# One more step between score products and value products in the mLSTM and retention chunks of a two-layer hybrid block

## The chip, the cores and the metric

The kernel runs on one core of a Trainium2 chip (trn2). The metric is device microseconds for one launch. TensorE multiplies matrices into PSUM, VectorE (DVE), ScalarE (ACT) and GpSimd (POOL) compute element by element, SyncE (SP) issues most of the DMAs. Each engine takes its own queue of instructions in the order in which it stands, and semaphores tie the queues to each other.

## The reference

Two layers of a block with three branches over 512 tokens of 1024 features, in fp32: an mLSTM, a sparse latent attention and a retention, each projected, gated and added, then a gated feed-forward. What the change touches are the chunks of 128 tokens of two branches:

```python
def mlstm step(carry, inp):                      # per chunk of 128 tokens, 4 heads
    sc = einsum('bhld,bhrd->bhlr', qc, kc) * w_intra
    num = einsum('bhlr,bhrv->bhlv', sc, vc) + w_inter * einsum('bhld,bhdv->bhlv', qc, c_st)
    out = num / max(|den|, exp(-m_row))
    c_new = decay * c_st + einsum('bhl,bhld,bhlv->bhdv', wk, kc, vc)

def retention step(state, inp):
    sc = einsum('bhld,bhrd->bhlr', qc, kc) * intra
    out = einsum('bhlr,bhrv->bhlv', sc, vc) + q_decay * einsum('bhld,bhdv->bhlv', qc, state)
    state = chunk_decay * state + einsum('bhrd,hr,bhrv->bhdv', kc, k_decay, vc)

hm = head_layer_norm(mlstm(...)) * sigmoid(m_o)
hr = head_layer_norm(retention(...)) * silu(r_g)
y = sigmoid(g_m) * (hm @ p_m) + sigmoid(g_a) * (ha @ p_a) + sigmoid(g_r) * (hr @ p_r)
```

## The kernel before, in words

The large products of the block are cut into **sections**: 512 columns of a weight matrix against all 512 tokens, in four PSUM banks named mm. A weight chunk of 256 rows is loaded by SyncE (L235) and split into a rounded high part (whi, ScalarE, L237) and the rest (wlo, VectorE, L238); three matmuls (L255 to L257) then make one product of nearly fp32 accuracy. A section with tokens on the output's partitions (`tok_section`) takes 24 matmuls per weight chunk and ends when its four banks are emptied: for RQ and RK, the query and key of the retention, by ScalarE into rz (L518); a section with features on the partitions (`feat_section`) for a gate by VectorE into sg (L487).

The smaller work of the branches runs **beside** these sections. A branch is a Python generator that issues instructions up to a `yield`; a section calls `tick` twice per weight chunk, and each tick advances a generator by its rate: the mLSTM by 0.75 steps per tick beside RQ, RK and RV (L536), the retention by 1.25 beside the first gate section GM (L562), each drained before the sections after them. Inside a branch four chunks of 128 tokens follow each other one step apart:

```python
def wave(gens, lag=1):
    active, gens, n = [], list(gens), 0
    while active or gens:
        if gens and n % lag == 0:
            active.append(gens.pop(0))
        n += 1
        for g in list(active):
            if next(g, active) is active:
                active.remove(g)
        yield
```

One step of an mLSTM chunk makes the score products (L854), masks them on VectorE into msc (L856) and makes the state product in two halves (L864, both in one PSUM tile), which VectorE adds to the old state (L866, once per half). The next step makes the value products (L877, and L879 against the state), divides by the normalizer (L881 to L884) and normalizes per head (`head_norm`): statistics on VectorE (L361, L362), an addition and a power on GpSimd (L312, L313), four L366 and a multiplication L368 on VectorE, all in place on mhx. Two empty steps later `to_T` turns the chunk with four transposes (L373) into one PSUM tile, which ScalarE rounds (L307) and VectorE subtracts (L308) into hmT, the operand of the projection p_m. The retention does the same with a step of its own ahead for its transposed query and key (L905, L907), with msc named rsc (L915), the products L913, L920, L930 and L932, a copy rhx (L934) and hrT.

The instructions of each engine are then put in order by a scheduler that goes by its own priorities; the code gives the dependencies, and a weight chunk's split and a section's evacuation are issued at high priority. Small PSUM tiles (sm) rotate over four banks. Beside the mLSTM also runs the top-k selection of the attention, pairs of L653 and L654 on VectorE (named top and mask).

Of the kernel before, what the change touches and what calls it, by code (L numbers as in the profile page):

```python
# [77 lines left out]
# [10 lines that stand above are left out]
# [17 lines left out]
class Block:  # L105
# [737 lines left out]
    def mlstm(self, qz, kT, v1, og, hmT):  # L843
        nc = self.nc
        W, G, qw, kw, dec = self.ml
        for v, x in enumerate(self.branch_T("hmT")):
            hmT[v] = x
        states = [None]

        def chunk(c):  # L850
            s = slice(c * 128, (c + 1) * 128)
            p = self.sm([128, 4, 128])
            for h in range(4):
                nc.tensor.matmul(p[:, h, :], lhsT=kT[h // 2][:, s], rhs=qz[:, h, s], start=True, stop=True)  # L854
            sc = self.r("msc", [4, 128])
            nc.vector.tensor_mul(sc, p, W[:, c])  # L856
            cst = states[c]
            if c < NT - 1:
                u = self.sm([128, 2, 129])
                new = self.r("mst", [2, 129])  # L860
                for hp in range(2):
                    for i in range(2):
                        h = 2 * hp + i
                        nc.tensor.matmul(u[:, hp, :], lhsT=kw[c][:, h, :], rhs=v1[:, c, h, :], start=i == 0, stop=i == 1)  # L864
                    if c:
                        nc.vector.scalar_tensor_tensor(new[:, hp, :], cst[:, hp, :], dec[:, hp, c:c + 1], u[:, hp, :],  # L866
                                                       op0=OP.mult, op1=OP.add)
                if c == 0:
                    nc.vector.tensor_copy(new, u)
                states.append(new)  # L870
            yield
            hx = self.r("mhx", [4, 128])
            for hp in range(2):
                o = self.sm([128, 2, 129])
                for i in range(2):
                    h = 2 * hp + i
                    nc.tensor.matmul(o[:, i, :], lhsT=sc[:, h, :], rhs=v1[:, c, h, :], start=True, stop=c == 0)  # L877
                    if c:
                        nc.tensor.matmul(o[:, i, :], lhsT=qw[:, h, s], rhs=cst[:, hp, :], start=False, stop=True)  # L879
                dn = self.stat(2, "mdn")  # L880
                nc.vector.tensor_tensor(dn, o[:, :, 128], G[:, 1, c, 2 * hp:2 * hp + 2], op=OP.max)  # L881
                nc.vector.scalar_tensor_tensor(dn, o[:, :, 128], -1.0, dn, op0=OP.mult, op1=OP.max)
                nc.vector.reciprocal(dn, dn)
                nc.vector.tensor_mul(hx[:, 2 * hp:2 * hp + 2, :], o[:, :, 0:128],  # L884
                                     dn[:, :, None].to_broadcast([128, 2, 128]))
            self.head_norm(hx, og[c])
# [3 lines that stand above are left out]
            self.to_T(hx, hmT, c)  # L890

        yield from wave(chunk(c) for c in range(NT))

    def retention(self, rq, rk, rv, rg, hrT):
        nc = self.nc
        for v, x in enumerate(self.branch_T("hrT")):
            hrT[v] = x
        states = [None]

        def chunk(c):  # L900
            T2 = []
            for n, x in (("rqT", rq), ("rkT", rk)):
                p = self.sm([128, 4, 128])
                for h in range(4):
                    nc.tensor.transpose(p[:, h, :], x[c][:, h, :], self.ident)  # L905
                y = self.r(n, [4, 128])
                nc.scalar.activation(y, p, AF.Copy)  # L907
                T2.append(y)
            qT, kT = T2
            yield  # L910
            p = self.sm([128, 4, 128])
            for h in range(4):
                nc.tensor.matmul(p[:, h, :], lhsT=kT[:, h, :], rhs=qT[:, h, :], start=True, stop=True)  # L913
            sc = self.r("rsc", [4, 128])
            nc.vector.tensor_mul(sc, p, self.c01[:, None, :].to_broadcast([128, 4, 128]))  # L915
            st = states[c]
            if c < NT - 1:
                u = self.sm([128, 4, 128])
                for h in range(4):
                    nc.tensor.matmul(u[:, h, :], lhsT=rk[c][:, h, :], rhs=rv[c][:, h, :], start=True, stop=True)  # L920
                new = self.r("rst", [4, 128])
                if c:
                    nc.vector.tensor_add(new, u, st)
                else:
                    nc.vector.tensor_copy(new, u)
                states.append(new)
            yield
            o = self.sm([128, 4, 128])
            for h in range(4):
                nc.tensor.matmul(o[:, h, :], lhsT=sc[:, h, :], rhs=rv[c][:, h, :], start=True, stop=c == 0)  # L930
                if c:
                    nc.tensor.matmul(o[:, h, :], lhsT=qT[:, h, :], rhs=st[:, h, :], start=False, stop=True)  # L932
            hx = self.r("rhx", [4, 128])
            nc.scalar.activation(hx, o, AF.Copy)  # L934
            self.head_norm(hx, rg[c])
# [3 lines that stand above are left out]
            self.to_T(hx, hrT, c)  # L939

        yield from wave(chunk(c) for c in range(NT))

    def ffn(self, l, X, act):
# [94 lines left out]
```

## Time and profile before

| what | value |
|---|---|
| median of three runs | 1820.44 us (1819.31 to 1820.54) |
| the profiled execution | 1819.63 us |
| its span in the profile | 1817.8 us |
| TensorE busy | 1789.1 us, 98% |
| VectorE busy | 981.1 us, 54% |
| ScalarE busy | 741.4 us, 41% |
| GpSimd busy | 218.8 us, 12% |

The span runs from the first instruction to the last; the execution's own time also has what lies around it. A wait is read in the timeline as the idle time in brackets behind a row, with the instruction that ended it. The mLSTM chunks of the first layer run from 133 to 175 us, the retention chunks from 237 to 273 us; in the second layer from 1031 to 1072 and from 1136 to 1172 us.

### The profile page before, as it was taken

What the parts mean: (1) busy time and instruction counts of PE and PEld (TensorE: products, weight loads), DVE (VectorE), ACT (ScalarE), POOL (GpSimd) and SP (SyncE); (2) the same over time, 40 slices, a digit from 0 to 9 for tenths busy, and PEclk for the clock granted to TensorE, in tenths of its full rate; (3) what the DMA queues carried; (4) which work ended last, traced back from release to release, by engine and by line L of the source; (5) the groups of instructions that cost most, each with busy time, mean ns of one, the idle gap of its engine ahead of it and who ended that gap; (6) DMA issues with size and microseconds to landing.
All of it is one profiled execution on the core that took longest, in us unless ns stands there. A gap on an engine that the chain in (4) does not pass through costs nothing.

```text
span 1817.8 us, 22873 instructions
## 1 busy us (share of the span) xinstructions
PE 1789.1 (98%) x8720; PEld 1491.1 (82%) x8720; DVE 981.1 (54%) x1799; ACT 741.4 (41%) x1208; POOL 218.8 (12%) x274
## 2 busy tenths in 40 slices
PE   9999999999999999999999999999999999999998
PEld 6878888878888888888887788888888888888886
DVE  5698985455545333322357999754546443333223
ACT  5572235656434323322246523366654333223221
POOL 3112240121000000000020132311210000000000
PEclk9999999999999999999999999999999999999999
DMA  6522323222235333222342223232223243332232
GB/s 188 203 83 81 115 72 100 89 91 87 81 128 162 93 95 102 93 96 102 102 131 70 76 85 101 68 112 80 90 70 137 87 158 95 94 105 93 94 103 81
DMA packets 126845, 185.95 MB, mean 102 GB/s; under 512 B 12256, under 2 KB 71136, under 8 KB 126736
## 3 DMA queue, kind: packets, MB, share of 16 engines
q1 hardware_dynamic: 125408, 178.98, 31.4%
q0 software_dynamic: 1184, 5.26, 0.8%
q8 instruction: 68, 1.11, 0.2%
q14 instruction: 41, 0.34, 0.1%
q10 hardware_dynamic: 144, 0.26, 0.0%
HBM read 177.64 MB, written 6.84 MB: 101 GB/s over the span
## 4 chain that ended last, share of the span: by engine, by line
PE 79%; DVE 13%; ACT 3%; issue 2%; DMA 2%; POOL 1%; SPq 0%; POOLq 0%; ACTq 0%; DVEq 0%
PE mm L255 23%; PE mm L257 23%; PE mm L256 23%; DVE wlo L238 3%; DVE mask L654 3%; DVE top L653 2%; PE sm L735 2%; PE sm L714 1%; PE sm L728 1%; ACT whi L237 1%; DVE ru L527 1%; PE sm L373 1%; PE sm L255 0%; PE sm L256 0%; DVE mhx L366 0%
## 5 line engine op out<-in xcount | busy, mean ns | idle before, releaser
L238 DVE TENSOR_TENSOR wlo<-raw,whi 128x1024 fp32r<-128x1024 f32 (+2 forms) x302 | 373.7, 1238 | 585.2 <-ACT whi L237 585.0
L237 ACT ACTIVATE whi<-raw 128x1024 fp32r<-128x1024 f32 (+2 forms) x302 | 314.0, 1040 | 709.1 <-PE mm L256 301.2
L255 PE MATMUL mm<-hT,whi 128*128 128x512 f32 (+1 forms) x1216 | 465.5, 383 | 0.1
L256 PE MATMUL mm<-hT,whi 128*128 128x512 f32 (+1 forms) x1216 | 460.4, 379 | 1.1 <-DVE hT L308 1.1
L257 PE MATMUL mm<-hT,wlo 128*128 128x512 f32 (+1 forms) x1216 | 460.9, 379 | 0.0
L257 PEld LDWEIGHTS mm<-hT,wlo 128*128 128x128 f32 x1216 | 228.8, 188 | 42.9
L256 PEld LDWEIGHTS mm<-hT,whi 128*128 128x128 f32 x1216 | 229.0, 188 | 42.0 <-DVE hT L308 1.7
L255 PEld LDWEIGHTS mm<-hT,whi 128*128 128x128 f32 x1216 | 229.0, 188 | 40.7 <-ACT rg L548 0.5
L255 PE MATMUL mm<-whi,hT 128*128 128x512 f32 (+1 forms) x448 | 177.0, 395 | 1.6 <-ACT hT L307 0.9
L257 PE MATMUL mm<-whi,hT 128*128 128x512 f32 (+1 forms) x448 | 174.8, 390 | 0.0
L256 PE MATMUL mm<-wlo,hT 128*128 128x512 f32 (+1 forms) x448 | 174.2, 389 | 0.0
L255 PEld LDWEIGHTS mm<-whi,hT 128*128 128x128 f32 x448 | 84.2, 188 | 18.7 <-ACT hT L307 1.6
L257 PEld LDWEIGHTS mm<-whi,hT 128*128 128x128 f32 x448 | 84.1, 188 | 18.0 <-issue 1.2
L256 PEld LDWEIGHTS mm<-wlo,hT 128*128 128x128 f32 x448 | 84.2, 188 | 16.1 <-issue 0.5
L325 POOL TENSOR_SCALAR rs<-ms 128x1 f32<-128x1 f32 x16 | 5.7, 354 | 620.4 <-ACT hn L323 620.4
L255 PE MATMUL mm<-whi,fa 128*128 128x512 f32 x192 | 74.7, 389 | 0.0
L256 PE MATMUL mm<-wlo,fa 128*128 128x512 f32 x192 | 74.7, 389 | 0.0
L257 PE MATMUL mm<-whi,fa 128*128 128x512 f32 x192 | 74.7, 389 | 0.0
L716 POOL TENSOR_TENSOR cmb<-tb,mask 128x256 f32<-128x256 f32 (+2 forms) x48 | 51.4, 1075 | 160.0 <-PE sm L728 54.5
L255 PE MATMUL mm<-whi,fr 128*128 128x512 f32 x160 | 62.4, 390 | 0.0
L257 PE MATMUL mm<-whi,fr 128*128 128x512 f32 x160 | 62.3, 389 | 0.0
L256 PE MATMUL mm<-wlo,fr 128*128 128x512 f32 x160 | 62.3, 389 | 0.0
(287 smaller groups left out, 2651.7 us busy)
## 6 DMA issues: line engine op xcount, KB each, us to landing
raw<-w_in SPq DMA_DIRECT2D x104, 512.0 KB, 3.6
raw<-w_gate SPq DMA_DIRECT2D x96, 256.0 KB, 2.8
raw<-w_up SPq DMA_DIRECT2D x96, 256.0 KB, 3.0
raw<-w_down SPq DMA_DIRECT2D x44, 512.0 KB, 3.5
raw<-w_out SPq DMA_DIRECT2D x16, 512.0 KB, 3.6
x<-x SPq DMA_DIRECT2D x8, 512.0 KB, 6.3
rot<-c_rot SPq DMA_DIRECT2D x16, 256.0 KB, 3.0
tb<-bias_dram SPq DMA_DIRECT2D x16, 256.0 KB, 3.8
```

What stands on the lines that cost most here:

```text
L237: nc.scalar.activation(h, r, AF.Copy)
L238: nc.vector.tensor_sub(o, r, h.bitcast(F32))
L255: t.matmul(out, lhsT=A[0], rhs=B[0], start=start, stop=False)
L256: t.matmul(out, lhsT=A[0], rhs=B[1], start=False, stop=False)
L257: t.matmul(out, lhsT=A[1], rhs=B[0], start=False, stop=stop)
L373: self.nc.tensor.transpose(p[:, h, :], x[:, h, :], self.ident)
L527: nc.vector.tensor_mul(u, z, sin)
L653: nc.vector.max(m8, acc)
L654: nc.vector.match_replace(acc, m8, acc, TAKEN)
L714: nc.tensor.matmul(p, lhsT=q[v][:, b * 128:(b + 1) * 128], rhs=kk[v][:, 0:SP], start=v == 0, stop=v == 1)
L716: nc.gpsimd.tensor_add(c, tb[:, T - S:T], masks[b] if b else self.neg)
L735: nc.tensor.matmul(o[:, b, :], lhsT=PT[:, s, :], rhs=V[s][:, h * 64:(h + 1) * 64], start=s == 0, stop=s == b)
```

## The change

Each chunk function gets one more `yield` between the step that makes the scores and the state and the step that makes the value products. Within a branch, one more set of score and state products is issued ahead of a chunk's value products; the branch takes one step more in all.

```diff
                     nc.vector.tensor_copy(new, u)
                 states.append(new)
             yield
+            yield
             hx = self.r("mhx", [4, 128])
             for hp in range(2):
                 o = self.sm([128, 2, 129])
@@ -924,6 +925,7 @@
                 else:
                     nc.vector.tensor_copy(new, u)
                 states.append(new)
+            yield
             yield
             o = self.sm([128, 4, 128])
             for h in range(4):
```

No engine gets more or fewer instructions; lines below the first added one count one higher in the changed kernel, below the second two. What the scheduler makes of it is shown at two places. In the rows, numbers behind a name are allocation counters; the chunks' normalized tiles are mhx_1358, 1422, 1512 and 1590 for mLSTM chunks 0 to 3 before, and mhx_1387, 1473, 1544 and 1604 in the change.

TensorE, first layer, mLSTM, end of the section RQ (mm_1284 to 1287) and start of RK (mm_1690 on), before:

```order
L257 MATMUL mm_1287<-whi_1566,hT11_125 128x512
L373 MATMUL sm_1643<-cm_84,mhx_1422 128x128 x4
L255 MATMUL mm_1690<-whi_1695,hT00_122 128x512
L256 MATMUL mm_1690<-wlo_1696,hT00_122 128x512
L257 MATMUL mm_1690<-whi_1695,hT10_124 128x512
```

Chunk 1's transposes stand there alone; chunk 2's stand 24 weight matmuls into RK, chunk 3's 12 further. The same place in the change (RK is mm_1683 on):

```order
L878 MATMUL sm_1615<-v1_430,msc_1517 128x129
L880 MATMUL sm_1615<-mst_1430,qw_1181 128x129
L373 MATMUL sm_1719<-cm_84,mhx_1473 128x128 x4
L373 MATMUL sm_1748<-cm_84,mhx_1544 128x128 x4
L255 MATMUL mm_1683<-whi_1688,hT00_122 128x512
L256 MATMUL mm_1683<-wlo_1689,hT00_122 128x512
L257 MATMUL mm_1683<-whi_1688,hT10_124 128x512
```

Chunk 3's value products (L878, L880) and the transposes of chunks 1 and 2 now stand right before RK's first matmul; between chunk 2's value products and its transposes stand 12 weight matmuls, chunk 0's transposes, chunk 3's value products and chunk 1's transposes.

ScalarE at the same place, before (sm_1583 and sm_1643 hold the transposed chunks 0 and 1):

```order
L307 ACTIVATE hmT0_1320<-sm_1583 128x4x128
L518 ACTIVATE rz_1656<-mm_1284 128x512
L518 ACTIVATE rz_1660<-mm_1285 128x512
L237 ACTIVATE whi_1781<-raw_1780 128x1024
L518 ACTIVATE rz_1664<-mm_1286 128x512
L518 ACTIVATE rz_1668<-mm_1287 128x512
L307 ACTIVATE hmT0_1320<-sm_1643 128x4x128
```

and in the change (sm_1597, 1719 and 1748 hold the transposed chunks 0, 1 and 2):

```order
L307 ACTIVATE hmT0_1320<-sm_1597 128x4x128
L307 ACTIVATE hmT0_1320<-sm_1719 128x4x128
L307 ACTIVATE hmT0_1320<-sm_1748 128x4x128
L518 ACTIVATE rz_1649<-mm_1284 128x512
L518 ACTIVATE rz_1653<-mm_1285 128x512
L518 ACTIVATE rz_1657<-mm_1286 128x512
L518 ACTIVATE rz_1661<-mm_1287 128x512
```

The rounding of chunks 1 and 2 moved ahead of the four evacuations of RQ.

VectorE, first layer, retention, end of the section GM, before (rhx_2490 is chunk 3):

```order
L362 BN_AGGR bmv_2493<-bst_2492 128x2 x2
L366 TENSOR_SCALAR rhx_2490<-rhx_2490,bmv_2493,lnr_2502 128x128 x4
L368 TENSOR_TENSOR rhx_2490<-rhx_2490,rg_1283 128x512
L308 TENSOR_TENSOR uvl_2609<-wuv_2607,uvh_2608 128x512
L308 TENSOR_TENSOR hrT1_2225<-sm_2522,hrT0_2224 128x4x128
L487 COPY sg_2198<-mm_2202 128x512
```

and in the change (rhx_2502 is chunk 3):

```order
L487 COPY sg_2198<-mm_2202 128x512
L362 BN_AGGR bmv_2505<-bst_2504 128x2 x2
L366 TENSOR_SCALAR rhx_2502<-rhx_2502,bmv_2505,lnr_2514 128x128
L487 COPY sg_2199<-mm_2203 128x512
L366 TENSOR_SCALAR rhx_2502<-rhx_2502,bmv_2505,lnr_2514 128x128 x3
L308 TENSOR_TENSOR hrT1_2225<-sm_2540,hrT0_2224 128x4x128
L487 COPY sg_2200<-mm_2204 128x512
L368 TENSOR_TENSOR rhx_2502<-rhx_2502,rg_1283 128x512
```

Three of the section's four evacuations and a split of a transposed chunk moved ahead of chunk 3's L368. TensorE there, the last transposes of the retention and the start of the projection p_m, before:

```order
L257 MATMUL mm_2205<-hT01_123,wlo_2531 128x512
L373 MATMUL sm_2566<-cm_84,rhx_2490 128x128 x4
L255 MATMUL mm_2581<-hmT0_1320,whi_2586 128x512
L256 MATMUL mm_2581<-hmT1_1321,whi_2586 128x512
L257 MATMUL mm_2581<-hmT0_1320,wlo_2587 128x512
```

Only chunk 3's transposes stand there; in the change:

```order
L257 MATMUL mm_2205<-hT01_123,wlo_2524 128x512
L373 MATMUL sm_2559<-cm_84,rhx_2454 128x128 x4
L373 MATMUL sm_2566<-cm_84,rhx_2502 128x128 x4
L255 MATMUL mm_2581<-hmT0_1320,whi_2586 128x512
L256 MATMUL mm_2581<-hmT1_1321,whi_2586 128x512
L257 MATMUL mm_2581<-hmT0_1320,wlo_2587 128x512
```

Chunk 2's transposes moved down to chunk 3's; between chunk 3's value products and its transposes stood 36 weight matmuls and two sets of transposes, and now stand 24 and two. The second layer's listings have the same shape at these places.

## Rows read from the trace of the kernel before

**Rows 1.** The page: TensorE's busy time over the span.

```profile
PE 1789.1 (98%) x8720; PEld 1491.1 (82%) x8720; DVE 981.1 (54%) x1799; ACT 741.4 (41%) x1208; POOL 218.8 (12%) x274
```

**Rows 2.** Timeline (start us, us, engine, line, work), TensorE: nineteen weight matmuls' first and last.

```profile
1805.91 0.39 PE L257 MATMUL mm<-whi,fr 128*128 128x512 f32 x1
...
1809.99 0.39 PE L257 MATMUL mm<-whi,fr 128*128 128x512 f32 x1
```

**Rows 3.** Timeline, TensorE: its waits in the chunk stages, in brackets.

```profile
139.72 1.16 PE L877 MATMUL sm<-v,msc 128*128 128x129 f32 x8 [0.89 <-DVE msc L856]
...
148.51 0.68 PE L864 MATMUL sm<-v,kw 128*128 128x129 f32 x4 [0.85 <-DVE mst L866]
...
245.07 1.16 PE L930 MATMUL sm<-rv,rsc 128*128 128x128 f32 x8 [1.05 <-DVE rsc L915]
...
1041.43 0.49 PE L877 MATMUL sm<-v,msc 128*128 128x129 f32 x2 [0.24 <-DVE msc L856]
...
1049.43 0.71 PE L864 MATMUL sm<-v,kw 128*128 128x129 f32 x4 [0.65 <-DVE mst L866]
...
1143.72 1.16 PE L930 MATMUL sm<-rv,rsc 128*128 128x128 f32 x8 [1.60 <-DVE rsc L915]
```

**Rows 4.** Timeline, TensorE: mLSTM chunks 2 and 3 and the transposes.

```profile
156.51 0.39 PE L879 MATMUL sm<-mst,qw 128*128 128x129 f32 x2
...
160.37 0.60 PE L373 MATMUL sm<-cm,mhx 128*128 128x128 f32 x4
160.80 0.39 PE L877 MATMUL sm<-v,msc 128*128 128x129 f32 x2
...
162.37 0.39 PE L879 MATMUL sm<-mst,qw 128*128 128x129 f32 x2
...
171.26 0.60 PE L373 MATMUL sm<-cm,mhx 128*128 128x128 f32 x4
...
1053.62 0.39 PE L879 MATMUL sm<-mst,qw 128*128 128x129 f32 x2
```

**Rows 5.** Timeline, VectorE: mLSTM chunk 2, its normalization.

```profile
157.08 1.21 DVE L238 TENSOR_TENSOR wlo<-raw,whi 128x1024 fp32r<-128x1024 f32 x1
...
159.46 0.67 DVE L856 TENSOR_TENSOR msc<-sm,mw 128x512 f32<-128x512 f32 x1
...
164.95 0.68 DVE L368 TENSOR_TENSOR mhx<-mhx,og 128x512 f32<-128x512 f32 x1
...
1062.41 0.68 DVE L368 TENSOR_TENSOR mhx<-mhx,og 128x512 f32<-128x512 f32 x1
```

**Rows 6.** Timeline, ScalarE: end of the section RQ.

```profile
161.00 0.60 ACT L307 ACTIVATE hmT<-sm 128x512 fp32r<-128x512 f32 x1 [4.79 <-PE sm L373]
161.50 1.08 ACT L518 ACTIVATE rz<-mm 128x512 f32<-128x512 f32 x2
```

**Rows 7.** Timeline, TensorE: the last value product of retention chunk 3.

```profile
263.35 0.39 PE L932 MATMUL sm<-rst,rqT 128*128 128x128 f32 x2
```

**Rows 8.** Timeline, VectorE and GpSimd: retention chunks 2 and 3.

```profile
262.30 1.12 DVE L366 TENSOR_SCALAR rhx<-rhx,bmv,lnr 128x128 f32<-128x128 f32 x4 [1.47 <-POOL lnr L313]
...
267.34 3.32 DVE L366 TENSOR_SCALAR rhx<-rhx,bmv,lnr 128x128 f32<-128x128 f32 x4 [1.47 <-POOL lnr L313]
270.69 0.69 DVE L368 TENSOR_TENSOR rhx<-rhx,rg 128x512 f32<-128x512 f32 x1
...
272.50 0.68 DVE L487 COPY sg<-mm 128x512 f32<-128x512 f32 x1
...
268.88 1.69 POOL L716 TENSOR_TENSOR cmb<-tb,mask 128x256 f32<-128x256 f32 x2
```

**Rows 9.** Windows (stretch: us; busy (instructions) of PE, PEld, DVE, ACT, POOL; granted TensorE clock; DMA share, GB/s).

```profile
1.30:6.30 5.00, 5.00 (x6) 2.17 (x7) 0.49 (x2) 2.50 (x4) 0.23 (x2) 1.00 0.88 280
6.40:9.00 2.60, 2.60 (x7) 1.09 (x6) 1.28 (x1) 0.88 (x1) 0.48 (x1) 1.00 1.06 397
...
1815.50:1817.70 2.20, 0.00 (x0) 0.00 (x0) 0.00 (x0) 0.00 (x0) 0.00 (x0) 0.50 0.38 155
```

## Prediction

> **What bounds the kernel now.** I read the page first. TensorE is busy for 98% of the span [rows 1], so the time is the length of TensorE's own queue plus the moments in which it stands still. I then took TensorE's rate from the timeline: between the two rows of [rows 2] lie 18 starts of a 512-column weight matmul in 4.08 us, so one costs 0.227 us. Nothing else that runs beside it has a price of its own; what counts is whether TensorE's next instruction finds its operand ready. The timeline of the two chunk stages shows where it does not [rows 3]: the value products wait for VectorE's masked scores at four places (0.89, 0.24, 1.05 and 1.60 us), and the second half of a state product waits for VectorE to have read the first half at two (0.85 and 0.65 us). Together that is **5.28 us**, and it is all that the extra step can win: it puts other work between scores and value products, so that VectorE has longer.
>
> **What the change moves.** No instruction is added or taken away. Each chunk's value products stand one step later, and with them all that follows in the chunk: the head normalization on VectorE and GpSimd, and the four transposes of its result (to_T). Both branches already end close to the end of the section that they run beside, and there the listings show what happened: the last transposes, which stood one at a time between weight matmuls, now stand together at the section's end, with fewer matmuls ahead of them. TensorE takes its queue in order, so if a normalized chunk is late, the weight matmuls behind its transposes wait too. So I compare, for the last transposes of each branch, TensorE's path from the end of that chunk's value products to its transposes with VectorE's chain from the same point to the end of the normalization (L368).
>
> **mLSTM, chunk 2, first layer.** The chain: the last value product ended at 156.51 + 0.39 = 156.90, L368 at 164.95 + 0.68 = 165.63, so 8.73 us [rows 4, 5]. Before, the transposes started at 171.26, 14.36 us after the products, and nothing waited. In the new order there stand between the two only 12 weight matmuls (12 x 0.227 = 2.72), chunk 0's transposes (160.37 to 160.80: 0.43), chunk 3's value products (160.80 to 162.37 and one step of 0.22: 1.79) and chunk 1's transposes (0.43). That is 5.37 us, less 0.16 because TensorE starts its next instruction that much before the record of the last one ends: 5.21. The chain does not get shorter: on VectorE, in the stretch between, a weight split (L238, 1.21 us) now stands where a score multiplication (L856, 0.67) stood, so I add 0.55: 9.28. **Wait: 9.28 - 5.21 = 4.1 us.** Behind it stands the first weight matmul of the next section (RK), which needs a PSUM bank that ScalarE empties (L518). ScalarE takes its queue in order too, and now all three transposed chunks (L307) stand ahead of the four L518. After the transposes it has to do one L307 (0.60) and one L518 (half of 1.08) [rows 6], and TensorE's last transpose ends 0.16 after the next could start: 1.3 us more. First layer: 5.4.
>
> **Second layer.** The same positions; the chain there is 1054.01 to 1063.09, or 9.08 us, so 9.08 + 0.55 - 5.21 = 4.4, and with the 1.3 for the bank 5.7.
>
> **Retention, chunk 3, both layers.** The last value product ended at 263.35 + 0.39 = 263.74 [rows 7] and L368 at 270.69 + 0.69 = 271.38: a chain of 7.64 us [rows 8]. In the new order 24 weight matmuls (5.45) and two sets of transposes (0.86) stand between, less 0.16: 6.15. That alone leaves 1.5 us of waiting. But the section that retention runs beside (the gate GM) ends here, and VectorE's evacuations of its four banks (L487, 0.68, or 0.60 from start to start) and two splits (L308) that stood behind L368 now stand ahead of it: one L487 among the statistics, one between the L366, and an L308 and an L487 right before L368. The L366 themselves are slow here: four take 3.32 us where they take 1.12 in the chunk before, and the last ends at 270.66, when GpSimd's run of adds ends (268.88 + 1.69 = 270.57) [rows 8]. If the L487 between them hides in that delay, the insertions cost 3 x 0.60 = 1.8 and the wait is 3.3; if it does not, and the splits ahead of the statistics hold these up by 0.2 as well, 2.4 + 0.2 and 4.1. No row decides; I take the middle, **3.7 us**, twice: the second layer's listing has the same order there.
> The Trainium skill ("SBUF — State Buffer", section "Who interferes with whom") says that VectorE and GpSimd share one port pair, which one of them holds for a whole instruction, and that a VectorE instruction with at most one SBUF input outside the two-port modes does not contend. By that rule the L487, which reads PSUM, runs on beside GpSimd while an L366 is blocked: 3.3 us, and the whole 0.8 us lower. The trace agrees with its first half (the L366 that ends with GpSimd's last add); no row has an L487 in such a place.
>
> **Sum.** New waits 5.4 + 5.7 + 3.7 + 3.7 = 18.5; waits that go, 5.28. The products' waits go because at least a second set of scores now lies between; those of the state products because VectorE no longer has a whole normalization ahead of L866. Net **+13.2 us**. The profiled execution took 1819.63 us, 0.8 below the median of the runs, so 1832.8 against its own time and **1834 us** beside a median of 1820.44.
> Bounds: with no insertion on VectorE adding anything the waits are 4.8, 5.1, 1.5 and 1.5, or 12.9, and the net is +7.6 (1828). With VectorE still 1 us late from chunk 1 when chunk 2's products come (they follow each other sooner now; the 1 us is my guess at that), 4.1 in retention, and the state products' 1.5 staying, it is 21.3 - 3.8 = +17.5 (1838).
>
> **The rivals.**
> First, the clock falls. TensorE was at 2.4 GHz from 6.4 us to the end of its work: in the first 5.00 us only six of the opening matmul records fit, in the next 2.60 seven, and the only fall in the trace, to 0.50, comes at 1815.4, some 5.0 us after the last matmul [rows 2, 9]. The waits that I expect, 3.3 to 4.4 us unbroken, and 5.7 with four transposes inside, are longer than any inside the kernel now, and just short of that. The opening cost about 2.5 us (5 us at half the rate); so 2.5 per fall, up to 10 for four: 1836.5 to 1844. For it: the mLSTM waits are nearly as long as the one that ended the clock. Against it: that one is the only fall that the rows have, and it is longer than each of mine.
> The Trainium skill ("TensorE: Matmul & The Clock Gate", section "What's actually happening") says that the slow clock is the default and that activity releases it; by that rule a long wait costs twice, once as a wait and once at 1.2 GHz after it. The trace agrees at both ends of the kernel; inside it, it shows no wait long enough to tell.
> Second, **faster**: the transposes find their chunk ready, and only the 5.28 us are left: 1820.4 - 5.3 = 1815. It needs VectorE to finish mLSTM's chunk 2 within 5.2 us of its products and retention's chunk 3 within 6.2. For it speaks that some top-k steps now run before the chunks; against it that from the score multiplication at 159.46 on the chain still took 6.17 us [rows 5], most of it statistics, GpSimd's power, the four L366 and L368, which must follow each other.
> Third, no visible change: the new waits are about as long as those that go (within 3.6 us, the 0.2% that a measurement of this kernel can tell from nothing). It needs them under 9 us together, below my lower bound of 12.9; this could be if the listing's positions mattered less than I think, as when TensorE is held up earlier and VectorE catches up.
>
> **How the numbers follow.** The forecast with the clock up gets 0.58, the falling clock 0.26, the faster case 0.04, the unchanged one 0.06; 0.06 is left for something larger that I do not see. The range 1827 to 1844 takes in both bounds of the sum and the falling clock. Faster by over 0.2%: 0.04; within 0.2%: 0.06; slower: 0.90.
>
> **What would show it.** In the profile after, the waits at L877, L930 and L864 (L878, L932 and L864 there) should be gone or under 0.5 us. At L373 TensorE should wait four times for L368: near 4 us on mhx in each layer, 3.3 to 4.1 on rhx, and after the first kind 1.3 us at the first weight matmul of RK, for ScalarE. VectorE's busy time should not change by more than some us. If L373 waits under 1 us everywhere, the chain argument is wrong. If the weight matmuls behind a wait start more than 0.4 us apart, the clock fell. If the time is lost elsewhere, in attention, say, the moved sections did it and not the transposes.

## The result, and the profile after

The changed kernel takes 1846.35 us (median of 4, 1843.94 to 1848.0) against 1819.88 for the kernel before, measured beside it: a ratio of 1.0143 with an interval of 1.0131 to 1.0156. It is **26.5 us slower**; 13.2 were forecast, and the time lies outside the range of 1827 to 1844.

The page's line of TensorE (busy us, share of the span, instructions; the span is 1844.4 us, the execution took 1846.2) answers to [rows 1]:

```profile
PE 1799.6 (98%) x8720; PEld 1499.3 (81%) x8720; DVE 979.3 (53%) x1799; ACT 742.5 (40%) x1208; POOL 214.9 (12%) x274
```

The span grew by 1844.4 - 1817.8 = 26.6 us. TensorE's idle time (span less busy) went from 1817.8 - 1789.1 = 28.7 to 1844.4 - 1799.6 = 44.8, which is **16.1 us more waiting**. The other **10.5 us are busy time**: 8720 instructions as before, but 1799.6 us instead of 1789.1. The same matmuls took longer.

The waiting first. The timeline of TensorE after (start, us, engine, line, work, and in brackets the idle time before it and what ended it), which answers to [rows 3]; the value products are L878 and L880 here and L932 and L934, the state product is still L864:

```profile
141.60 0.60 PE L864 MATMUL sm<-v,kw 128*128 128x129 f32 x3 [0.97 <-DVE mst L866]
...
169.92 0.88 PE L373 MATMUL sm<-cm,mhx 128*128 128x128 f32 x4 [5.04 <-DVE mdn L882]
171.98 0.79 PE L255 MATMUL mm<-whi,hT 128*128 128x512 f32 x1 [1.17 <-ACT rz L518]
...
283.84 1.09 PE L373 MATMUL sm<-cm,rhx 128*128 128x128 f32 x4 [3.93 <-DVE rhx L368]
...
1053.26 0.71 PE L864 MATMUL sm<-v,kw 128*128 128x129 f32 x4 [0.35 <-DVE mst L866]
...
1075.72 0.46 PE L878 MATMUL sm<-v,msc 128*128 128x129 f32 x2 [0.47 <-DVE mdn L883]
...
1081.75 1.09 PE L373 MATMUL sm<-cm,mhx 128*128 128x128 f32 x4 [4.46 <-DVE mdn L882]
1084.01 0.79 PE L255 MATMUL mm<-whi,hT 128*128 128x512 f32 x1 [1.17 <-ACT rz L518]
...
1195.56 0.87 PE L373 MATMUL sm<-cm,rhx 128*128 128x128 f32 x3 [3.89 <-DVE rhx L368]
```

The four waits of transposes and the two at RK's first matmul are where they were expected: 5.04 + 1.17 + 4.46 + 1.17 + 3.93 + 3.89 = 19.66 us. The value products wait for their masked scores nowhere any more. Of the 5.28 us of [rows 3], 0.97 + 0.35 = 1.32 us are left, both at the state product; the 0.47 at L878 is another wait, whose bracket names an instruction on the products of the chunk before (L883). So 19.66 + 1.32 + 0.47 - 5.28 = 16.2 us more, which is the page's 16.1.

Then the busy time. Windows of the timeline after (columns as in [rows 9]; the 0.50 or 1.00 is the granted clock):

```profile
164.80:169.90 5.10, 0.09 (x1) 0.01 (x1) 4.17 (x13) 0.60 (x1) 2.37 (x3) 1.00 0.36 103
170.20:176.90 6.70, 5.53 (x16) 4.06 (x15) 5.21 (x18) 2.56 (x5) 2.58 (x4) 0.50 0.13 36
177.10:183.80 6.70, 6.70 (x31) 5.50 (x31) 6.46 (x12) 1.06 (x1) 4.22 (x4) 1.00 0.31 81
282.90:289.60 6.70, 5.76 (x16) 4.73 (x17) 3.72 (x6) 1.64 (x3) 1.57 (x1) 0.50 0.08 22
...
1081.60:1088.30 6.70, 5.38 (x14) 4.13 (x15) 5.46 (x22) 2.55 (x5) 3.00 (x4) 0.50 0.13 39
1194.20:1200.90 6.70, 5.34 (x15) 4.41 (x16) 4.14 (x7) 1.63 (x3) 1.56 (x1) 0.50 0.08 22
```

Around the end of each of the four long waits the clock stands at 0.50, the 1.2 GHz level, and TensorE gets 14 to 16 instructions through 6.70 us, in which it also idles for 0.9 to 1.4 us; in the same length right behind the first it gets 31 through at 1.00. In the first the clock was still up inside the wait (the window from 164.80 on); in the other three it had fallen before the wait was over, since their windows start ahead of the transposes. The weight matmuls behind the first wait start 0.43 us apart, where they start 0.227 apart in [rows 2]:

```profile
172.57 0.63 PE L256 MATMUL mm<-wlo,hT 128*128 128x512 f32 x1
173.00 0.63 PE L257 MATMUL mm<-whi,hT 128*128 128x512 f32 x1
```

That is the first rival of the prediction, by its own sign (more than 0.4 us apart), at all four places. The busy time puts its price at 10.5 / 4 = **2.6 us a fall**.

What makes the transposes late is VectorE's chain, with GpSimd's power in it. The first layer's mLSTM: the last value product of chunk 2 on TensorE, and from there on VectorE's rows (which answer to [rows 4, 5]):

```profile
159.12 0.39 PE L880 MATMUL sm<-mst,qw 128*128 128x129 f32 x2
```

```profile
160.23 1.12 DVE L366 TENSOR_SCALAR mhx<-mhx,bmv,lnr 128x128 f32<-128x128 f32 x4 [1.10 <-POOL lnr L313]
...
161.38 0.69 DVE L368 TENSOR_TENSOR mhx<-mhx,og 128x512 f32<-128x512 f32 x1
...
165.32 1.21 DVE L238 TENSOR_TENSOR wlo<-raw,whi 128x1024 fp32r<-128x1024 f32 x1
167.47 1.11 DVE L366 TENSOR_SCALAR mhx<-mhx,bmv,lnr 128x128 f32<-128x128 f32 x4 [0.93 <-POOL lnr L313]
168.50 0.68 DVE L308 TENSOR_TENSOR hmT<-sm,hmT 128x512 fp32r<-128x512 f32 x1
169.10 0.68 DVE L368 TENSOR_TENSOR mhx<-mhx,og 128x512 f32<-128x512 f32 x1
```

The products end at 159.12 + 0.39 = 159.51, but until 161.38 + 0.69 = 162.07 VectorE is mostly at chunk 1, whose L366 waited for GpSimd's power; the chunk's own L368 ends at 169.10 + 0.68 = 169.78. Its chain took 10.27 us, where it took 8.73 before. The transposes start 0.14 us later. The bracket names L882, the next instruction in VectorE's queue; in the second layer and in retention the start is the same 0.15 us behind the end of L368, so it is L368 that releases them. Two thirds of the 1.54 us by which the chain grew are GpSimd's: its power, after and then before,

```profile
165.36 2.07 POOL L313 TENSOR_TENSOR lnr<-lnr,mhalf 128x4 f32<-128x4 f32 x1
```

```profile
162.24 1.04 POOL L313 TENSOR_TENSOR lnr<-lnr,mhalf 128x4 f32<-128x4 f32 x1
```

takes 1.03 us longer where VectorE's split L238 (165.32) starts beside it; before, a split stood ahead of the chunk's statistics (157.08 in [rows 5]).

The second layer's mLSTM, the last value product of chunk 2 on TensorE and the chunk's L368:

```profile
1070.81 0.39 PE L880 MATMUL sm<-mst,qw 128*128 128x129 f32 x2
```

```profile
1080.91 0.69 DVE L368 TENSOR_TENSOR mhx<-mhx,og 128x512 f32<-128x512 f32 x1
```

Here the power took its usual 1.03 us and the chain 1081.60 - 1071.20 = 10.40, where it took 9.08 before: VectorE starts on chunk 2's products (L882) only at 1073.85, and the split L238 stands among the statistics. TensorE's own path to the transposes was longer too, 1081.75 - 4.46 - 1071.20 = 6.09 us against 5.37 in the first layer, in part since the 0.47 at L878 lies in it.

Retention, first layer, VectorE and GpSimd in chunk 3 (answering to [rows 8]); the last value product on TensorE:

```profile
273.10 0.39 PE L934 MATMUL sm<-rst,rqT 128*128 128x128 f32 x2
```

```profile
273.97 0.68 DVE L308 TENSOR_TENSOR uvl<-wuv,uvh 128x512 fp32r<-128x512 f32 x1
274.57 0.68 DVE L308 TENSOR_TENSOR hrT<-sm,hrT 128x512 fp32r<-128x512 f32 x1
275.17 0.47 DVE L361 BATCH_NORM_STATS2 bst<-rhx 128x6 f32<-128x128 f32 x2
...
276.08 0.67 DVE L487 COPY sg<-mm 128x512 f32<-128x512 f32 x1
...
278.39 0.63 DVE L366 TENSOR_SCALAR rhx<-rhx,bmv,lnr 128x128 f32<-128x128 f32 x1 [1.48 <-POOL lnr L313]
278.65 0.68 DVE L487 COPY sg<-mm 128x512 f32<-128x512 f32 x1
279.25 2.65 DVE L366 TENSOR_SCALAR rhx<-rhx,bmv,lnr 128x128 f32<-128x128 f32 x3
...
283.02 0.67 DVE L368 TENSOR_TENSOR rhx<-rhx,rg 128x512 f32<-128x512 f32 x1
```

```profile
278.41 1.09 POOL L694 MEMSET kl<- 64x512 f32 x2
```

From 273.10 + 0.39 = 273.49 to the end of L368 at 283.02 + 0.67 = 283.69 it took 10.20 us where it took 7.64 before. The statistics start 275.17 - 273.49 = 1.68 us behind the products, where they started 264.66 - 263.74 = 0.92 behind them before:

```profile
264.66 0.48 DVE L361 BATCH_NORM_STATS2 bst<-rhx 128x6 f32<-128x128 f32 x2
```

The two splits (L308) now hold them up, and two of the evacuations (L487) shown stand inside the normalization; an L308 and a third L487 stand in the gap left out ahead of L368. GpSimd's own work (L694, then L716) runs beside the L366.

### The profile page after: what moved, and what is told of

The parts are those of the page before. It is cut to its first block, busy times and chain, and to the rows that moved or that the text cites. A ratio compares the mean times of both kernels' runs of the same rounds, so it can differ in the third digit from the quotient of the medians.

```text
span 1844.4 us, 22900 instructions
## 1 busy us (share of the span) xinstructions
PE 1799.6 (98%) x8720; PEld 1499.3 (81%) x8720; DVE 979.3 (53%) x1799; ACT 742.5 (40%) x1208; POOL 214.9 (12%) x274
## 4 chain that ended last, share of the span: by engine, by line
PE 83%; DVE 8%; ACT 3%; issue 2%; DMA 2%; POOL 1%; SPq 0%; POOLq 0%; ACTq 0%; DVEq 0%
PE mm L255 25%; PE mm L257 25%; PE mm L256 25%; PE sm L735 2%; DVE wlo L238 1%; PE sm L714 1%; PE sm L728 1%; POOL lnr L313 1%; ACT whi L237 1%; DMA raw<-w_up 1%; DVE rhx L366 1%; PE sm L373 1%; DVE mask L654 1%; DVE bst L361 1%; DVE top L653 0%
## 5 line engine op out<-in xcount | busy, mean ns | idle before, releaser
L238 DVE TENSOR_TENSOR wlo<-raw,whi 128x1024 fp32r<-128x1024 f32 (+2 forms) x302 | 373.6, 1237 | 614.6 <-ACT whi L237 599.1
L716 POOL TENSOR_TENSOR cmb<-tb,mask 128x256 f32<-128x256 f32 (+2 forms) x48 | 52.0, 1087 | 161.0 <-PE sm L728 54.5
```

The source lines that it names most:

```text
L238: nc.vector.tensor_sub(o, r, h.bitcast(F32))
L716: nc.gpsimd.tensor_add(c, tb[:, T - S:T], masks[b] if b else self.neg)
```

## The experiments

Each kernel was timed beside the kernel before on the same chip. The theory: the late value products make the normalization late, TensorE waits for it in front of the next section, and the clock falls at each such wait. The medians of the kernel before were 1819.58 us for the first four runs, 1820.29 for the next four and 1819.97 for the last two.

### The two branches apart

One added `yield` each:

```diff
@@ mLSTM only: def mlstm, ahead of the value products
             yield
+            yield
             hx = self.r("mhx", [4, 128])
@@ retention only: def retention, ahead of the value products
             yield
+            yield
             o = self.sm([128, 4, 128])
```

> The extra step in the mLSTM chunks alone. Theory (late normalization, then half a clock): of the waits after, mLSTM's stay: 5.0 and 4.5 us at the transposes, twice 1.2 at RK's first matmul, 1.8 at L864 and L878; of those before 2.6 go. Net +11.0, and two falls of the clock of 6.83 us, of which 1.17 is idle, cost (6.83 - 1.17) / 2 = 2.8 each: +16.6 us, near 1836.5. Rival (waits alone, the clock costs nothing that counts): +11, near 1831. Rival (the two branches make each other late): under +8, since neither is late alone.

> The extra step in the retention chunks alone. Theory: waits of 3.9 us at the transposes twice, 2.65 go at the value products: net +5.2, and two falls, each 6.83 us of which about 1 is idle, cost 2.9 each: +11 us, near 1831. With mLSTM alone the two should add up to the whole change, 26 to 28 us. Rival (waits alone): +5, near 1825. Rival (the branches make each other late): under +3, and the two do not add up.

Measured: mLSTM alone 1832.55 us (1.0072, 1.0055 to 1.0089), +13.0; retention alone 1830.98 us (1.0063, 1.0048 to 1.0078), +11.4. Together 24.4, against 26.5 for both. TensorE's line of the page of mLSTM alone (span 1830.5), then of retention alone (span 1828.2):

```profile
PE 1793.3 (98%) x8720; PEld 1495.3 (82%) x8720; DVE 981.3 (54%) x1799; ACT 741.9 (41%) x1208; POOL 214.9 (12%) x274
```

```profile
PE 1793.1 (98%) x8720; PEld 1493.2 (82%) x8720; DVE 978.2 (54%) x1799; ACT 741.4 (41%) x1208; POOL 221.7 (12%) x274
```

Idle time rose by 37.2 - 28.7 = 8.5 us and 35.1 - 28.7 = 6.4, busy time by 4.2 and 4.0. The waits are those of the whole change: 5.05 and 4.46 at mLSTM's transposes, and in retention alone, on TensorE's timeline:

```profile
276.10 0.63 PE L373 MATMUL sm<-cm,rhx 128*128 128x128 f32 x4 [3.92 <-DVE rhx L368]
...
1148.58 0.68 PE L913 MATMUL sm<-rqT,rkT 128*128 128x128 f32 x4 [1.73 <-DVE rsc L915]
```

So each branch pays for its own late chunk, and neither needs the other for it. mLSTM came out 3.6 us under what was expected: its two falls cost 4.2 us, not 5.6, and retention's old waits at L930 (2.65 us) happened not to occur, though nothing was changed there. The wait in the second layer of retention alone is 3.91. There part of the old waiting came back at the score products (L913, ended by L915). The clock stood at 0.50 for 3.4 us at each of its two waits, where it was 6.8 at each of the whole change's four. Why, no run says.

### Keeping TensorE at work in the waits

The changed kernel, with products of constants that are overwritten by the transposes:

```diff
-    def to_T(self, x, hT, t):
-        p = self.sm([128, 4, 128])
+    def to_T(self, x, hT, t, fill=0):
+        p = self.sm([128, 4, 128]); [self.nc.tensor.matmul(p.rearrange("p h d -> p (h d)"), lhsT=self.ident, rhs=self.cm, start=True, stop=True) for _ in range(fill)]
...
-            self.to_T(hx, hmT, c)
+            self.to_T(hx, hmT, c, 2 if c == 2 else 0)
...
-            self.to_T(hx, hrT, c)
+            self.to_T(hx, hrT, c, 4 if c == 3 else 0)
```

> The changed kernel, with matmuls of constants put right before the transposes that wait, into the same PSUM tile, which the transposes then overwrite: two in mLSTM chunk 2 (some 1.7 us), four in retention chunk 3 (some 3.4 us). Theory: the transposes start when they did (the normalization ends when it did), TensorE idles 2.8 to 3.3 us there in mLSTM and about 0.5 in retention. In retention the clock stays up: 2 x 2.9 = 5.8 us less than the changed kernel, near 1840.5; if the clock stays up in mLSTM too, 11.4 less, near 1835. Rival (the clock falls for another reason than the idle time, or costs nothing): no change from the changed kernel, 1846; the falls stay where they are. Rival (the added matmuls hold up something else): over 1846.

Measured: 1839.83 us (1.0109, 1.0094 to 1.0125), 20.3 us above the kernel before, where the change was 26.5 above: 6.2 us less. The intervals of the two ratios do not overlap. TensorE's timeline (L371 are the added products):

```profile
169.28 3.78 PE L371 MATMUL sm<-cm 128*128 128x512 f32 x4 [4.31 <-DVE hmT L308]
172.86 1.06 PE L373 MATMUL sm<-cm,mhx 128*128 128x128 f32 x4
...
283.11 0.66 PE L373 MATMUL sm<-cm,rhx 128*128 128x128 f32 x4 [0.39 <-DVE rhx L368]
...
1075.69 1.98 PE L371 MATMUL sm<-cm 128*128 128x512 f32 x4 [1.63 <-DVE hmT L308]
1078.43 0.66 PE L373 MATMUL sm<-cm,mhx 128*128 128x128 f32 x4 [0.75 <-DVE mhx L368]
```

and its windows at the first three of the four places (columns as above; the fourth reads as the second):

```profile
167.10:173.80 6.70, 4.52 (x9) 2.34 (x10) 6.29 (x26) 0.47 (x1) 0.58 (x3) 0.50 0.26 78
282.50:289.20 6.70, 6.31 (x30) 5.11 (x30) 3.49 (x5) 2.33 (x4) 2.10 (x1) 1.00 0.07 22
1078.50:1085.20 6.70, 5.53 (x26) 4.44 (x27) 5.46 (x21) 2.56 (x5) 3.01 (x4) 1.00 0.13 42
```

At three places the transposes still wait for the same L368 (0.36 us at the last of them), so nothing was won on the chain; but there the wait was filled or broken up, and the clock stayed at 1.00. Three falls at 2.6 us would be 7.9; this trace has one short fall that no other run's trace has, behind a wait of 1.95 us at the feed-forward's L350. The remaining place, mLSTM in the first layer, is informative by failing: there the added products themselves waited 4.31 us, for L308, the clock was at 0.50 before they started (the window from 167.10 on), and they held the transposes up to 172.86, past the end of L368. They need nothing but the PSUM tile, so **a second condition** stands almost as late as the chunk: the tile of chunk 0's transposes, which VectorE empties with an L308 that stands in its queue right before the chunk's L368 (168.50 in the rows of after).

### Later transposes, unmoved value products

```diff
             self.head_norm(hx, og[c])
             yield
             yield
+            yield
             yield
             self.to_T(hx, hmT, c)
```

and the same in the retention.

> The kernel before, with the extra step not before the value products but after them, ahead of the transposes: these stand one step later, at the same section ends as in the change, while value products and normalization stay where they were. Theory (it is the late value products, and with them the late normalization, that make TensorE wait): no wait over 1 us at L373, no fall of the clock, within 2 us of the kernel before. Rival (it is the transposes, brought together at the section's end with fewer matmuls ahead of them): +10 us or more, with waits of 3 us or more at L373 for L368.

Measured: 1817.44 us (0.9991, 0.9982 to 1.0001), 2.1 us less than the kernel before. TensorE's timeline (the last transposes of mLSTM, then those of retention):

```profile
177.20 0.60 PE L373 MATMUL sm<-cm,mhx 128*128 128x128 f32 x4
...
270.93 1.03 PE L373 MATMUL sm<-cm,rhx 128*128 128x128 f32 x8
```

Nothing waits at L373, and the clock does not fall there; at L930 0.80 us are left, in the second layer. In retention the transposes of chunks 2 and 3 stand together at the section's end (x8), as in the change, and cost nothing there, since their chunks were ready: the moved value products do the harm, not the grouping. In mLSTM the scheduler spread the transposes into RK (from 164.86 to 177.20 us), so for that branch this run doesn't tell the two apart.

### Without the late normalization

```diff
-            self.head_norm(hx, og[c])
+            if c != 2: self.head_norm(hx, og[c])
...
-            self.head_norm(hx, rg[c])
+            if c != 3: self.head_norm(hx, rg[c])
```

on top of the change.

> The changed kernel without the head normalization of the four late chunks: head_norm is left out for mLSTM chunk 2 and retention chunk 3 in both layers, their raw chunks are transposed. Theory (TensorE waits there for the end of the normalization on VectorE): in retention the waits of 3.9 us go entirely, with the clock falls there. In mLSTM a wait stays, since the PSUM tile of the transposes is that of chunk 0, which VectorE frees (L308) behind a weight split (L238): 2 to 3.5 us instead of 5.0 and 4.5, plus the 1.2 at RK. Waits less by 7.8 + 3 to 5; of the 10.5 us by which TensorE's busy time rose, 5 to 10.5 go: 1823 to 1831. Rival (the transposes wait for something else, or come too late for their place): waits stay within 0.5 us of 5.0, 4.5, 3.9, 3.9, and the time within 3 us of the changed kernel's 1846.

Measured: 1825.81 us (1.0026, 1.0014 to 1.0038). TensorE's timeline:

```profile
167.47 1.11 PE L373 MATMUL sm<-cm,mhx 128*128 128x128 f32 x4 [2.26 <-DVE hmT L308]
...
276.79 1.03 PE L373 MATMUL sm<-cm,rhx 128*128 128x128 f32 x8
...
1069.39 0.66 PE L373 MATMUL sm<-cm,mhx 128*128 128x128 f32 x4 [1.34 <-DVE hmT L308]
1071.22 0.50 PE L255 MATMUL mm<-whi,hT 128*128 128x512 f32 x1 [1.17 <-ACT rz L518]
```

Retention's waits and falls are gone, and mLSTM's shrank to the second condition, L308, 2.26 and 1.34 us (the second is shorter than expected). The kernel is 5.5 us above the kernel before instead of 26.5: 21 us went with four normalizations. Both waits of mLSTM still lost the clock; for the whole kernel TensorE's busy time was 1793.3 us.

### Room at the section's end

Four kernels ask whether the extra step costs by itself or only where a section ends too soon. The edits beside the added `yield`:

```diff
@@ retention that may sink: retention only, and
-            self.to_T(hx, hrT, c)
+            with self.tc.high_priority(offset=-100): self.to_T(hx, hrT, c)
@@ slow mLSTM: mLSTM only, and
-        self.during((ml, 0.75), (top, 1.5))
+        self.during((ml, 0.5), (top, 1.5))
@@ two steps: the change, and in both branches, ahead of to_T
             yield
+            yield
             self.to_T(hx, hmT, c)
```

> The extra step in the retention alone, and the retention's transposes at a lower priority, so that weight matmuls of p_m and of the section after it go ahead of the last ones. Theory (the step costs only because the next section stands behind the late transposes): no wait over 1 us at L373 for rhx, no fall of the clock; the value products' waits of 1.05 and 1.60 go, but the score products of 1.7 at L913 in the second layer, seen in the run with the retention alone, may stay. 1817 to 1822, 9 to 14 less than that run's 1831. Rival (the late hrT then holds up what reads it, or the wait moves to another place for the same chunk): 1827 or more, with a new wait of 3 us or more.

> The extra step in the mLSTM alone, and its steps fed more slowly beside the sections, 0.5 per tick where it was 0.75: the branch reaches past RQ into RK, and its four sets of transposes stand 24 weight matmuls (5.5 us) apart. Theory (the step costs only where chunks are pressed together at a section's end): no L373 wait over 1 us, no fall, 1817 to 1824, some 10 less than the 1832.5 of mLSTM alone. Rival (a chunk's normalization is too late by itself wherever it stands, since VectorE is loaded): waits of 2 us or more at L373 stay, 1828 or more.

> The changed kernel with one more empty step between normalization and transposes in both branches. Theory (steps that are left at a section's end are run out at once, so a step gives no time there): the waits of 3.5 to 5.5 us and the four falls stay, 1840 to 1850. Rival (the step gives VectorE the time that it lacks): waits at L373 under 1 us, no fall, 1816 to 1824.

**Retention that may sink**: 1822.55 us (1.0011, 1.0001 to 1.0020), 0.5 above what was expected. No wait at L373, no fall; the transposes of the last chunks stand from 288.69 us on, after p_m's first matmuls. What is left comes from the score products again (L913, 1.5 us in all) and from a DMA that L683 now waits for longer (2.1 us in all, 0.5 before).

**Slow mLSTM**: 1820.37 us (1.0001, 0.9992 to 1.0011). Its transposes stand at 174.87, 183.34, 189.27 and 195.20 us, nothing waits there, and the waits that the step was to remove turn up again at the value products (L877, 1.54 us the longest), now with L883 in the bracket, an instruction on earlier value products; that it is their PSUM tile that is waited for is not shown.

**Two steps**: 1839.15 us (1.0101, 1.0084 to 1.0117), a little under what was expected. The waits stay, in the first layer

```profile
170.61 1.11 PE L373 MATMUL sm<-cm,mhx 128*128 128x128 f32 x4 [5.29 <-DVE hmT L308]
```

and 3.36 at retention's (its start at 281.97 is again 0.14 us behind the end of L368), in the second 4.82 and 3.33; the clock fell at each. A step that falls behind the section's last tick gives no time. What this kernel has less than the change are the two waits of 1.17 at RK and some 0.5 us at each of retention's transposes; that doesn't explain all of the 7 us between the medians. The profiled execution took 1842.1, and its trace shows one more fall, near the start (0.50 from 11.2 to 14.5 us); why, no run says.

Last, both remedies at once, and the late transposes once more:

```diff
@@ both with room: the change, and
-        self.during((ml, 0.75), (top, 1.5))
+        self.during((ml, 0.5), (top, 1.5))
...
-            self.to_T(hx, hrT, c)
+            with self.tc.high_priority(offset=-100): self.to_T(hx, hrT, c)
```

> The change in both branches, with room at both ends: mLSTM's steps at 0.5 per tick as in the run with the slow mLSTM, the retention's transposes at the lower priority of the run where they sink. Theory (the whole loss is the late transposes ahead of the next section and the clock after them): no wait over 1 us at L373, no fall, and the two runs' differences from before (+0.1 and +2.3) add up: 1819 to 1824. Rival (the extra step costs something of its own in the two together, as by chunks that meet): 1827 or more. Third (the extra step, freed of its cost, shows the gain of the 5.3 us that went): 1817 or less.

> The same kernel as in the first run with the late transposes, in more rounds: its first difference was -0.09% with an interval from -0.18% to +0.01%. If the wait at the value products that went there in the first layer (1.05 us) and the half of that in the second are all, -1.5 to -2.5 us, near 1818; if the first run was chance, within 1 us of before.

Both with room: 1824.41 us (1.0025, 1.0015 to 1.0036), at the upper edge of what the theory gave. So 22 of the 26.5 us were the late transposes and the clock, and the extra step itself brings nothing even without them. In the place of the products' 5.28 us TensorE waits in that kernel, among others, 2.4 us at L683 for a DMA, 2.1 at L877 for L883 and 1.9 at L913 for L915.

Late transposes again: 1817.54 us (0.9989, 0.9980 to 0.9997), 2.4 us less than the kernel before. It is the only kernel here whose interval lies below the kernel before, by less than the 0.2% of the prediction; 1.7 us of it are waits at retention's value products (0.98 us in the second layer for 1.60, none in the first for 1.05).

## Why the prediction was wrong

**Right: the sign, the places and the mechanism.** The six new waits stand at the six instructions named, and the chain of VectorE against TensorE's path decides them: taking four normalizations out took 21 us away, and late transposes whose chunks are ready cost nothing. Retention's wait was given as 3.7 within 3.3 to 4.1 and is 3.93 and 3.89; RK's 1.3 is 1.17. The second layer's mLSTM, 4.46 for 4.4, is luck: the chain was put at 9.63 and took 10.40, TensorE's path was put at 5.37 and took 6.09, and the two errors cancel. VectorE's busy time did not change by more than 2 us.

**The step that failed is the choice between the forecast and the first rival.** The prediction held with 0.58 that the clock stays up, because the one fall in the rows followed a stretch longer than each of the new waits. So the sum put the clock's cost at nothing. The runs show it falling at all four, at 10.5 us of busy time, 2.6 a fall. That the rival's 2.5 us came so near is in part luck: it was taken from the pace of the opening matmuls, in a window whose granted clock reads 1.00 [rows 9], and no row showed how long the clock would stay down behind a wait. The run that keeps TensorE at work shows that it was these waits: broken up, they did not lose the clock. The row of 5.0 us only showed that such a stretch suffices; it was read as if shorter ones did not. The rule of the Trainium skill ("TensorE: Matmul & The Clock Gate", section "What's actually happening") that was weighed there, the slow clock as the default that activity releases, is what these rows agree with.

**The waits were mis-sized by 2.9 us, inside their bounds.** The sum was +13.2 with an upper bound of +17.5, and measured +16.1.
- mLSTM in the first layer: 5.04, not 4.1. The chain was put at 9.28 and took 10.27; TensorE's path, 169.92 - 5.04 - 159.51 = 5.37, was as put. The missing 1.0 is GpSimd's power, 2.07 us for 1.04. The 0.55 added for L238 is about the rest of the growth, but for another reason: L238 ran beside the power, behind the statistics, and these ended 0.5 us later because VectorE was still at chunk 1 when chunk 2's products came. The upper bound had a guess of 1.0 for that alone; in the sum it stood at nothing.
- State and value products: the sum had nothing left; 1.32 us stayed at L864 and 0.47 came at L878. The reason given, that no whole normalization stands ahead of L866 any more, did not suffice: at the 0.97 us none does, and VectorE is busy with masks (L856) and top-k steps instead.
- Retention: the total is nearly right, its parts are not. The L487 between the L366 was taken to cost between nothing and 0.60; the four L366 span 281.90 - 278.39 = 3.51 us with it and 3.32 without [rows 8], so it cost 0.2. The L487 takes its usual 0.68 beside GpSimd's L694; the rule of the Trainium skill ("SBUF — State Buffer", section "Who interferes with whom"), by which it does not contend, agrees with this row. But the splits ahead of the statistics cost more than the 0.2 allowed: these start 1.68 - 0.92 = 0.76 us later behind the products.

**And the range.** Its upper end took the falling clock on top of the middle of the sum, 1834 + 10 = 1844. On top of its upper bound, 1838, it would have been 1848, and that holds the result. Nothing in the rows kept the two from coming together.

**Rivals two and three** found no support: 1815 needed chunks that are ready, and they were 4 to 5 us late.

## What to carry to other kernels

Work that is fed step by step beside a section ends with that section; a step added early in it pushes its last pieces against the section's end, where the first matmul of the next one queues behind them. So ask of an added step not what it hides but what comes last, and compare the chain there with the work that is left to cover it. A link of that chain can take longer only because of what it now runs beside, as the power did here. A wait of several us on TensorE is to be priced twice: once as idle time, and once as slower matmuls at its end, which show up as busy time and not as a wait.

## What was not expected of the hardware

- **The clock's cost is invisible in the waits.** Between the kernels before and after, 10.5 of 26.6 us appear only as a busier TensorE with the same 8720 instructions. A profile read by its idle times alone would miss two fifths of the loss.
- **No single length of wait tells whether the clock falls.** Waits of 1.34 us and, four transposes later, 1.17, with 0.50 and 0.18 shortly before, lost it (the run without late normalization, second layer: TensorE got 10 instructions through the 3.30 us from 1071.95 on, at 0.50); 1.63, 0.75 and 1.17 with products between did not (the run with added products, second layer, 26 instructions in 6.70 us at 1.00); nor did 1.73 alone (retention alone, L913). What else decides is left open.
- **GpSimd's power takes twice as long beside one VectorE instruction.** In the twelve traces the power of a head normalization (L313 on lnr) took 1.03 to 1.05 us at 178 places and 2.06 to 2.13 at ten; at these ten, and at no other, a split L238 starts within 0.05 us of it. No run varied this by itself.
- **Left open**: in the kernel with room for both, TensorE's busy time is 1791.0 us, 1.9 above the kernel before, without a fall; no run says why.
